# Down-projection of a ConvGLU feed-forward: 38 of its 44 k-tiles by one level of Strassen's algorithm

## The chip, the cores and the metric

One Trainium2 chip, one of its cores. The metric is device time in microseconds from start to end of one execution; lower is better. The three runs of the kernel before have a median of 2918.61 us (2916.6 to 2919.67). Engines are called PE (TensorE, matrix products into PSUM), DVE (VectorE), ACT (ScalarE), POOL (GpSimd) and SP (SyncE, which here issues the transfers).

## The reference

One layer of a streaming encoder: adaLN-modulated RMSNorm, gated linear attention and gated DeltaNet, an output projection, then a ConvGLU feed-forward and a last RMSNorm. The change concerns the second product of the feed-forward and what follows:

```python
D_MODEL = 2048; D_FF = 5632; SEQ = 512; DEC_SEQ = 64

def conv_ffn(h, st, w_up, ffn_conv_w, ffn_conv_b, w_down):
    gate, val = jnp.split(h @ w_up, 2, axis=-1)
    gate_c, new_st = causal_dwconv(gate, st, ffn_conv_w)
    act = jax.nn.silu(gate_c + ffn_conv_b) * val
    return act @ w_down, new_st
...
        f, s_f = conv_ffn(h, ffn_s[l], w_up[l], ffn_conv_w[l], ffn_conv_b[l], w_down[l])
        x = x + g2 * f
...
    y = rmsnorm(x, final_norm)
```

It runs for 512 frames of a prompt and 64 frames of a sample, all in float32. So the down-projection multiplies 576 frames by a matrix of 5632 x 2048.

## The kernel before, in words

Activations lie with the model dimension on the 128 partitions and the frames along the free dimension, in two halves of 288 columns (256 of the prompt, 32 of the sample). w_down falls into 44 k-tiles (128 rows of D_FF) and 16 m-tiles (128 columns of D_MODEL).

A float32 product is made of three products of a reduced type (F32R): each operand is split into a high half (ACT copies it into F32R) and a low half (DVE subtracts the high half from the original). mm6 (L551) does one k-tile of one m-tile for both halves of the frames, six matmuls of 128 x 128 by 128 x 288: high weights with high activations, high weights with low ones, low weights with high ones.

up (L1437) is the stage ahead. It makes 44 tiles of the activation and uses one level of Strassen's algorithm (in Winograd's form) already. For each of the 44 tiles it works through seven products (up_product, L1362), each of 8 pairs of k-tiles and 24 matmuls, and prepares the weights of a product two products ahead (up_prep, L1332: DVE sums of raw weights, then the split by ACT and DVE). The results of a tile pass through buffers "cb", "ca" and "v" for the short convolution (up_conv, L1419) and the gate (up_act, L1425), and are written to DRAM tiles actd.

down (L1480) goes through the 44 k-tiles in 11 groups of four. acts (L1468) loads the four activation tiles of a group from actd into places that the up-projection's operands left free, and splits them; the next group's are loaded in the middle of a group, the first group's before the up-projection ends. For each pair of m-tiles, wtile (L652, through split, L638) loads 4 x 128 x 256 weights (512 KB) and splits them. Each m-tile takes 24 matmuls into a PSUM tile of two banks, of which there are two (pgt, L575), and residual (L1147) then adds the sum, times the adaLN gain, onto x1 in SBUF (two DVE operations, 512 and 64 columns). The 16 tiles of x1 are loaded from DRAM (xd) at the start of down. The eleventh group is done by final (L1511), one half of the frames after the other, with the last RMSNorm (final_part, L1574) between the products.

The order of instructions on each engine is set by a scheduler when the program is built: by the order in which they are written, where an instruction's inputs and buffers are there, and ahead of that order where they are there sooner. So the first activations and weights of down are fetched while up still runs. A buffer of a given tag is handed on when all its readers are done.

## Time and profile before

| | before |
|---|---|
| median of 3 runs | 2918.61 us |
| profiled execution, own time | 2917.59 us |
| its span (first to last instruction) | 2915.8 us |
| mean granted TensorE clock | 0.994 |
| PE instructions (matmuls) | 21052 |
| DVE instructions | 3543 |
| ACT instructions | 2118 |
| DMA traffic | 399.84 MB, 137 GB/s on average |

The span is the stretch of the profiled execution from its first to its last instruction; the execution's own time is 1.8 us longer, and the median of the timed runs 1.0 us longer than that. In the trace, the up-projection's matmuls run from 1311.7 to 2331.5 us, those of the down-projection's first ten groups begin at 2331.7 us, and the last group ends at 2901.5 us. A line number in a group of instructions is that of the kernel before; a busy PE is not a PE at its peak, since matmuls overlap.

### The profile page before, as it was taken

The numbers are of one execution on the slowest core, as the hardware profiler recorded it, in microseconds if no ns is written. First come the engines' busy times: TensorE is split into PE (matmuls) and PEld (weight loads), VectorE is DVE, ScalarE is ACT, GpSimd is POOL, SyncE is SP. The second block draws the span as 40 slices with busy tenths as digits, with TensorE's granted clock in tenths as the row PEclk, the third lists the DMA queues.
The fourth block names the chain that finished last, engine by engine and source line by source line (L and its number), as shares of the span: only waits on it lengthen the run. The fifth ranks groups of instructions, "written<-read, shape, count | busy, mean of one in ns | idle before, by whom it ended". The sixth has DMA issues, their size and how long they took to land.

```text
span 2915.8 us, 52420 instructions
## 1 busy us (share of the span) xinstructions
PE 2865.9 (98%) x21052; PEld 2766.4 (95%) x21052; DVE 2133.5 (73%) x3543; ACT 1239.9 (43%) x2118; POOL 321.0 (11%) x587
## 2 busy tenths in 40 slices
PE   7999999999999999999999999999999999999998
PEld 3599999999999999999999999999999999999997
DVE  5788878777777786468887888887888855555555
ACT  6574566544433233354444444444444422222223
POOL 0015432234210001000000000000000000000000
PEclk8999999999999999999999999999999999999999
DMA  8975555555456548333333333333333553333221
GB/s 302 302 205 148 157 154 159 155 140 165 124 149 174 145 144 250 113 104 106 107 100 105 106 107 106 107 99 106 105 106 107 175 185 102 114 102 113 87 81 66
DMA packets 511879, 399.84 MB, mean 137 GB/s; under 512 B 45865, under 2 KB 437764, under 8 KB 511636
## 3 DMA queue, kind: packets, MB, share of 16 engines
q1 hardware_dynamic: 506212, 385.82, 44.5%
q0 software_dynamic: 5424, 10.68, 1.1%
q8 instruction: 166, 2.72, 0.4%
q14 instruction: 77, 0.63, 0.1%
HBM read 356.27 MB, written 40.13 MB: 136 GB/s over the span
## 4 chain that ended last, share of the span: by engine, by line
PE 90%; DVE 4%; ACT 3%; DMA 2%; issue 1%; POOL 0%; SPq 0%; ACTq 0%; DVEq 0%; POOLq 0%
PE g L560 30%; PE g L562 15%; PE g L1372 9%; PE g L1373 8%; PE g L1374 8%; PE bank L1373 3%; PE bank L1372 3%; PE bank L1374 3%; PE bank L161 1%; DVE acc L819 1%; PE bank L825 1%; PE bank L433 1%; PE bank L752 1%; DVE wl L649 1%; PE bank L756 1%
## 5 line engine op out<-in xcount | busy, mean ns | idle before, releaser
L560 PE MATMUL g<-slot,wh 128*128 128x288 f32 x3168 | 551.4, 295 | 0.2 <-DVE slot L1150 0.2
L1372 PE MATMUL g<-slot,wh 128*128 128x290 f32 x1760 | 533.6, 303 | 3.0 <-ACT p L1384 2.6
L648 ACT ACTIVATE wh<-raw 128x1024 fp32r<-128x1024 f32 x239 | 253.0, 1059 | 658.5 <-PE g L560 622.5
L1373 PE MATMUL g<-slot,wh 128*128 128x290 f32 x1760 | 525.4, 299 | 0.0
L1374 PE MATMUL g<-slot,wl 128*128 128x290 f32 x1760 | 520.6, 296 | 0.0
L560 PEld LDWEIGHTS g<-slot,wh 128*128 128x128 f32 x3168 | 464.5, 188 | 0.7 <-DVE slot L1150 0.5
L560 PE MATMUL g<-hh,wh 128*128 128x288 f32 x1984 | 449.8, 306 | 2.3 <-ACT hh L1159 1.0
L560 PE MATMUL g<-hl,wh 128*128 128x288 f32 x1984 | 431.9, 297 | 0.0
L562 PE MATMUL g<-hh,wl 128*128 128x288 f32 x1984 | 431.5, 298 | 0.0
L1150 DVE SCALAR_TENSOR_TENSOR slot<-g,mod,slot 128x512 f32<-128x512 f32 (+1 forms) x448 | 201.8, 491 | 286.9 <-PE g L562 286.0
L1319 ACT ACTIVATE wh<-raw 128x1024 fp32r<-128x1024 f32 x176 | 186.8, 1061 | 390.2 <-PE g L1373 380.0
L1372 PEld LDWEIGHTS g<-slot,wh 128*128 128x128 f32 x1760 | 331.2, 188 | 17.6 <-ACT p L1384 11.7
L562 PE MATMUL g<-slot,wl 128*128 128x288 f32 x1584 | 341.7, 294 | 0.0
L1374 PEld LDWEIGHTS g<-slot,wl 128*128 128x128 f32 x1760 | 336.5, 191 | 0.0
L1373 PEld LDWEIGHTS g<-slot,wh 128*128 128x128 f32 x1760 | 335.6, 191 | 0.1
L649 DVE TENSOR_TENSOR wl<-raw,wh 128x1024 fp32r<-128x1024 f32 x239 | 291.4, 1220 | 52.2 <-ACT wh L648 51.3
L560 PEld LDWEIGHTS g<-hh,wh 128*128 128x128 f32 x1984 | 318.6, 190 | 5.5 <-ACT hh L1159 1.3
L560 PEld LDWEIGHTS g<-hl,wh 128*128 128x128 f32 x1984 | 320.9, 189 | 0.3
L562 PEld LDWEIGHTS g<-hh,wl 128*128 128x128 f32 x1984 | 319.4, 189 | 0.2 <-issue 0.2
L562 PEld LDWEIGHTS g<-slot,wl 128*128 128x128 f32 x1584 | 255.1, 188 | 0.0
L819 DVE SCALAR_TENSOR_TENSOR acc<-xr,ct,acc 128x512 f32<-128x512 f32 x322 | 230.3, 750 | 1.7 <-DMA xr<-in_w_ada_dram 1.7
L1320 DVE TENSOR_TENSOR wl<-raw,wh 128x1024 fp32r<-128x1024 f32 x176 | 214.7, 1220 | 18.3 <-ACT wh L1319 18.1
(373 smaller groups left out, 4540.5 us busy)
## 6 DMA issues: line engine op xcount, KB each, us to landing
raw<-in_w_up_dram SPq DMA_DIRECT2D x176, 512.0 KB
raw<-in_w_in_dram SPq DMA_DIRECT2D x108, 512.0 KB
raw<-in_w_down_dram SPq DMA_DIRECT2D x88, 512.0 KB
xr<-in_w_ada_dram SPq DMA_DIRECT2D x86, 512.0 KB
ax<-in_w_ada_dram SPq DMA_DIRECT2D x42, 512.0 KB
hraw<-in_w_ada_dram SPq DMA_DIRECT2D x40, 512.0 KB
raw<-in_w_out_dram SPq DMA_DIRECT2D x32, 512.0 KB
slot<-actd SPq DMA_DIRECT2D x44, 288.0 KB
```

Source lines behind the costliest of these rows:

```text
L161: self.nc.tensor.transpose(ps[:, b * P:(b + 1) * P], src4[:, b], self.c["ident"])
L560: T.matmul(ps[:, h if bank is None else bank, :n], wh, x[:, h, :n], start=f, stop=False)
L562: T.matmul(ps[:, h if bank is None else bank, :n], wl, ah[:, h, :n], start=False, stop=stop)
L648: nc.scalar.activation(hi[:, :n_], raw[:, :n_], AF.Copy)
L649: nc.vector.tensor_tensor(lo[:, :n_], raw[:, :n_], hi[:, :n_].bitcast(F32), op=ALU.subtract)
L819: V.scalar_tensor_tensor(acc[s], w[:, k], col, acc[s], op0=ALU.mult, op1=ALU.add)
L1150: self.nc.vector.scalar_tensor_tensor(x1[:, :, z], ps[:, :, c], gain[:, q:q + 1], x1[:, :, z], op0=ALU.mult, op1=ALU.add)
L1319: self.nc.scalar.activation(hi, src, AF.Copy)
L1320: self.nc.vector.tensor_tensor(lo, src, hi.bitcast(F32), op=ALU.subtract)
L1372: T.matmul(ps, wh[:, j], hi, start=(c < 3 and j == 0), stop=False, skip_group_check=True)
L1373: T.matmul(ps, wh[:, j], lo, start=False, stop=False, skip_group_check=True)
L1374: T.matmul(ps, wl[:, j], hi, start=False, stop=(j == NPAIR - 1), skip_group_check=True)
```

## The change

Two k-tiles (FIRST) are done as before, 38 as 19 pairs by Strassen's algorithm, and the last four by final as before. A pair is k-tile 2 + j and k-tile 21 + j; together with the two halves of the frames and the two halves of the m-tiles they make blocks of two by two, which seven products replace where eight would be needed. The pairs come in five groups of 3, 4, 4, 4 and 4; within a group the outputs are done in four quarters (two m-tiles of the upper and two of the lower half), and a quarter takes seven products. A product has n pairs x 2 m-tiles x 3 matmuls (24 with four pairs), summed in one PSUM bank per m-tile.

- Weights: down_load fetches four raw tiles of a quarter; DVE makes four sums of them (down_first, down_prep), and seven splits by ACT and DVE follow (down_split), two products ahead.
- Activations: down_pair makes seven combinations from the two tiles of a pair and splits each (put). The pairs of the next group are made in a group's third and fourth quarter, after the products that the code names. act_load brings activations in through the buffers "cb", "v" and "ca" of the up-projection (stage) and no longer through places of their own.
- Outputs: instead of being scaled and added onto x1 at once, the sums are gathered unscaled in SBUF (acc, and e0 for the part that three of four outputs share) by DVE (down_out). In the last group down_finish loads x from xd (four transfers a call), adds e0, scales by the gain on ACT (g2, negative for the lower half, whose sums have the other sign) and adds x. For the first two k-tiles ACT copies the sums from PSUM to acc.
- final adds its four k-tiles onto acc (final_sum) and reads its outputs there (xf).

```diff
...
 B11, T2, T1, B21, T3, B22, T4 = range(7)
+FIRST, NDOWN, GROUPS = 2, 19, (3, 4, 4, 4, 4)
...
-    def put(self, c, j, src, place=None):
+    def put(self, c, j, src, place=None, w=HZ):
         place = place or self.places.pop(0)
-        t = self.slot(place, F32R)
+        t = self.slot(place, F32R, w)
         self.split_z(t[:, 0], t[:, 1], src)
         self.combos[c, j] = t[:, 0], t[:, 1], place
...
+    def stage(self):
+        n = self.n_stage = self.n_stage + 1
+        tag = ("v", "cb", "v", "ca")[n % 4]
+        return self.ub.tile([P, 2, HZ], F32, tag=tag, bufs=2 if tag == "v" else 1, name=self.name("raw"))[:, :, :HT]
+    def act_load(self, t):
+        raw = self.stage()
+        self.nc.sync.dma_start(raw, self.actd[t])
+        return raw
+    def act_split(self, raw):
+        hh, hl = [self.slot(self.places.pop(0), F32R, HT) for _ in range(2)]
+        self.nc.scalar.activation(hh, raw, AF.Copy)
+        self.nc.vector.tensor_tensor(hl, raw, hh.bitcast(F32), op=ALU.subtract)
+        return hh, hl
+    def pair_load(self, j):
+        return [self.act_load(FIRST + j + half * NDOWN) for half in range(2)]
+    def down_pair(self, j, raws):
+        V = self.nc.vector
+        (b11, b12), (b21, b22) = [(r[:, 0], r[:, 1]) for r in raws]
+        put = lambda c, b: self.put(c, j, b, None, HT)
+        put(B11, b11)
+        V.tensor_tensor(b11, b11, b12, op=ALU.subtract)
+        put(T1, b11)
+        t = self.ub.tile([P, HZ], F32, tag=("p1", "r")[j % 2], name=self.name("t3"))[:, :HT]
+        V.tensor_tensor(t, b22, b12, op=ALU.subtract)
+        V.scalar_tensor_tensor(b12, b11, -1.0, b22, op0=ALU.mult, op1=ALU.subtract)
+        put(T2, b12)
+        put(T3, t)
+        put(B21, b21)
+        V.scalar_tensor_tensor(b21, b12, -1.0, b21, op0=ALU.mult, op1=ALU.subtract)
+        put(B22, b22)
+        put(T4, b21)
+    def down_rows(self, g, half):
+        k = FIRST + half * NDOWN + sum(GROUPS[:g])
+        return k, k + GROUPS[g]
...
+    def down_sum(self, step, c):
+        g, q = step
+        n = GROUPS[g]
+        return self.ua.tile([P, 1024], F32, tag=f"s{c}", name=self.name("s"))[:, :n * 256].rearrange("p (k n) -> p k n", k=n)
+    def down_first(self, step):
+        s1 = self.a[(*step, "s1")] = self.down_sum(step, 1)
+        self.nc.vector.tensor_tensor(s1, self.a[(*step, "a21")], self.a[(*step, "a22")], op=ALU.add)
+    def down_split(self, src):
+        k = src.shape[1]
+        hi, lo = [self.wq.tile([P, 1024], F32R, tag="w" + c, bufs=3, name=self.name("w" + c))[:, :k * 256]
+                  .rearrange("p (k n) -> p k n", k=k) for c in "hl"]
+        self.nc.scalar.activation(hi, src, AF.Copy)
+        self.nc.vector.tensor_tensor(lo, src, hi.bitcast(F32), op=ALU.subtract)
+        return hi, lo
+    def down_prep(self, step, c, following):
+        V, a = self.nc.vector, self.a
+        g = lambda n: a[(*step, n)]
+        if c == 0:
+            w = self.down_split(g("a11"))
+            s2 = a[(*step, "s2")] = self.down_sum(step, 2)
+            V.tensor_tensor(s2, g("s1"), g("a11"), op=ALU.add)
+        elif c == 1:
+            w = self.down_split(g("s2"))
+        elif c == 2:
+            w = self.down_split(g("s1"))
+            if following:
+                self.down_load(following, ("a21", "a22"))
+        elif c == 3:
+            w = self.down_split(g("a12"))
+        elif c == 4:
+            V.tensor_tensor(g("a21"), g("a11"), g("a21"), op=ALU.add)
+            w = self.down_split(g("a21"))
+            if following:
+                self.down_load(following, ("a11", "a12"))
+        elif c == 5:
+            V.tensor_tensor(g("s2"), g("a12"), g("s2"), op=ALU.add)
+            w = self.down_split(g("s2"))
+        else:
+            w = self.down_split(g("a22"))
+            if following:
+                self.down_first(following)
+        a[(*step, "w", c)] = w
+    def down_product(self, step, c):
+        T, (wh, wl) = self.nc.tensor, self.a.pop((*step, "w", c))
+        g = step[0]
+        if c == 0:
+            x, y, z = self.pgt(), self.pgt(), [self.bank() for _ in range(2)]
+            self.sums = x[:, :, :HT], y[:, :, :HT], [b[:, :HT] for b in z]
+            self.banks = [[x[:, a, :HT], y[:, a, :HT], z[a][:, :HT]] for a in range(2)]
+        j0, n = sum(GROUPS[:g]), GROUPS[g]
+        for a in range(2):
+            ps = self.banks[a][(0, 1, 2, 0, 1, 2, 1)[c]]
+            f = slice(a * P, (a + 1) * P)
+            for j in range(n):
+                hi, lo, _ = self.combos[c, j0 + j]
+                T.matmul(ps, wh[:, j, f], hi, start=(c < 3 and j == 0), stop=False, skip_group_check=True)
+                T.matmul(ps, wh[:, j, f], lo, start=False, stop=False, skip_group_check=True)
+                T.matmul(ps, wl[:, j, f], hi, start=False, stop=(j == n - 1), skip_group_check=True)
+    def down_out(self, step, c):
+        V, (g, q) = self.nc.vector, step
+        x, y, z = self.sums
+        if c == 0 and g == 0:
+            self.nc.scalar.activation(self.e0[q], x, AF.Copy)
+            return
+        out = (self.e0[q], self.acc[0, 1][q], self.acc[1, 1][q], self.acc[0, 0][q],
+               self.acc[1, 1][q], self.acc[0, 1][q], self.acc[1, 0][q])[c]
+        if c in (2, 5):
+            for a in range(2):
+                V.tensor_tensor(out[:, a], z[a], out[:, a], op=ALU.add)
+        else:
+            V.tensor_tensor(out, (x, y)[(0, 1, 2, 0, 1, 2, 1)[c]], out, op=ALU.add)
+    def down_finish(self, row, h, q):
+        nc, t = self.nc, self.acc[row, h][q]
+        xt = self.stage()
+        for a in range(2):
+            for c, z in ((slice(0, HP), slice(0, HP)), (slice(HP, HT), slice(ZS, HZ))):
+                nc.sync.dma_start(xt[:, a, c], self.xd[8 * row + 2 * q + a][:, h, z])
+        if row + h:
+            yield
+            nc.vector.tensor_tensor(t, t, self.e0[q], op=ALU.add)
+        yield
+        for a in range(2):
+            for n, c in enumerate((slice(0, HP), slice(HP, HT))):
+                nc.scalar.activation(t[:, a, c], t[:, a, c], AF.Copy, scale=self.g2[:, 8 * row + 2 * q + a, n:n + 1])
+        yield
+        nc.vector.tensor_tensor(t, t, xt, op=ALU.add)
     def down(self):
+        A = self.nc.scalar
         free = [self.combos[c, j][2] for c in range(7) for j in range(NPAIR)]
         take = lambda n: [free.pop(0) for _ in range(n)]
...
+        self.combos, self.a, self.n_stage = {}, {}, 0
         self.raw = self.raw_late
...
+        self.places = firsts = take(2 * FIRST)
+        firsts = list(firsts)
+        acts = [self.act_split(self.act_load(k)) for k in range(FIRST)]
+        self.places = take(7 * GROUPS[0])
+        quarters = lambda places: [self.slot(p, F32, HT) for p in places]
+        self.acc = {}
+        for row in range(2):
+            for h in range(2):
+                self.acc[row, h] = quarters(take(4))
+        self.e0_places = take(4)
+        self.e0 = quarters(self.e0_places)
+        self.places += free + firsts
+        self.g2 = self.sp.tile([P, KD, 2], F32, tag="g2", bufs=1, name="g2")
+        for half, f in ((0, 1.0), (1, -1.0)):
+            A.activation(self.g2[:, 8 * half:8 * half + 8], self.mod[:, 5, 8 * half:8 * half + 8], AF.Copy, scale=f)
+        steps = [((g, q), c) for g in range(len(GROUPS)) for q in range(4) for c in range(7)]
+        blocks = [b for b, c in steps if c == 0] + [None]
+        prep = lambda n: self.down_prep(*steps[n], blocks[n // 7 + 1]) if n < len(steps) else None
+        raws = {0: self.pair_load(0)}
+        for m0 in range(0, KD, 4):
+            wh, wl = self.wtile(self.i["w_down"][0, :FIRST * P, m0 * P:(m0 + 4) * P].rearrange("(k p) n -> p k n", p=P))
+            if m0 == 4:
+                self.down_load(blocks[0], ("a21", "a22"))
+            if m0 == 8:
+                self.down_load(blocks[0], ("a11", "a12"))
+                self.down_first(blocks[0])
+            for m in range(m0, m0 + 4):
+                ps = self.pgt()
+                c = slice((m - m0) * P, (m - m0 + 1) * P)
+                for k in range(FIRST):
+                    self.mm6(ps, wh[:, k, c], wl[:, k, c], acts[k], k == 0, k == FIRST - 1)
+                for h in range(2):
+                    A.activation(self.acc[m // 8, h][m % 8 // 2][:, m % 2], ps[:, h, :HT], AF.Copy, scale=(1.0, -1.0)[m // 8])
+            j = m0 // 4
+            if j < GROUPS[0]:
+                raws[j + 1] = self.pair_load(j + 1)
+                self.down_pair(j, raws.pop(j))
+        for n in range(2):
+            prep(n)
+        j, last, tasks = GROUPS[0], len(GROUPS) - 1, []
+        acts, loads = [], list(range(NFF - 4, NFF))
+        for n, (step, c) in enumerate(steps):
+            g, q = step
+            prep(n + 2)
+            self.down_product(step, c)
+            self.down_out(step, c)
+            if q == 3:
+                self.places += [self.combos[c, sum(GROUPS[:g]) + i][2] for i in range(GROUPS[g])]
+            if g < last and (q, c) in ((2, 0), (3, 1), (3, 3), (3, 5)):
+                if j + 1 < NDOWN:
+                    raws[j + 1] = self.pair_load(j + 1)
+                self.down_pair(j, raws.pop(j))
+                j += 1
+            if g == last:
+                if q == 0 and c < 4:
+                    loads[c] = self.act_load(loads[c])
+                if q == 0 and 1 < c < 6:
+                    acts.append(self.act_split(loads[c - 2]))
+                if c > 2:
+                    tasks.append(self.down_finish(*((0, 0), (1, 1), (0, 1), (1, 0))[c - 3], q))
+                for t in tasks[:2]:
+                    if next(t, self) is self:
+                        tasks.remove(t)
+        for t in tasks:
+            for _ in t:
+                pass
+        self.final(acts, self.places + [])
...
+    def xf(self, m, h):
+        return self.acc[m // 8, h][m % 8 // 2][:, m % 2]
+    def final_sum(self, ps, m, h):
+        x = self.xf(m, h)
+        for n, c in enumerate((slice(0, HP), slice(HP, HT))):
+            self.nc.vector.scalar_tensor_tensor(x[:, c], ps[:, m % 2, c], self.mod[:, 5, m, n:n + 1], x[:, c], op0=ALU.mult, op1=ALU.add)
...
+        free += self.e0_places
...
-                self.residual(ps[:, m % 2:m % 2 + 1], self.x1[m][:, h:h + 1], self.mod[:, 5, m])
+                self.final_sum(ps, m, h)
...
```

46 lines of the change are left out of this document (13 added, 33 removed).

## The prediction

> **What bounds the kernel now.** I read the page first (busy time and the chain that ended last), then the table of stretches for the two stages that the change joins, then the waits inside the down-projection.
>
> ```profile
> span 2915.8 us, 52420 instructions
> ...
> PE 2865.9 (98%) x21052; PEld 2766.4 (95%) x21052; DVE 2133.5 (73%) x3543; ACT 1239.9 (43%) x2118; POOL 321.0 (11%) x587
> ...
> PE 90%; DVE 4%; ACT 3%; DMA 2%; issue 1%; POOL 0%; SPq 0%; ACTq 0%; DVEq 0%; POOLq 0%
> ```
>
> TensorE carries 90% of the chain. In the stretches below the columns are stretch, length, PE, PEld, DVE, ACT and POOL busy, the granted clock, DMA share and GB/s. The first row lies in the up-projection, which already uses one level of Strassen, the second in the down-projection of today.
>
> ```profile
> 1800.00:2000.00 200.00, 200.00 (x1462) 197.02 (x1461) 163.17 (x200) 89.69 (x106) 15.16 (x27) 1.00 0.37 106
> 2500.00:2600.00 100.00, 100.00 (x759) 100.00 (x758) 53.28 (x88) 22.03 (x24) 0.00 (x0) 1.00 0.35 109
> ```
>
> TensorE never rests in either. VectorE and ScalarE wait for it (us in total, times, longest):
>
> ```profile
> ACT wh L648 <- PE g L560: 340.7, 67, 5.3
> DVE slot L1150 <- PE g L562: 222.4, 135, 2.2
> ```
>
> So a removed matmul is worth its full pitch, as long as VectorE, 53% busy here and 82% in the up-projection, can pay for it.
>
> **What is removed.** The down-projection has 44 x 16 x 6 = 4224 matmuls. After the change there are 2 x 16 x 6 = 192 (two k-tiles first), 19 pairs x 4 quarters x 7 products x 2 x 3 = 3192, and 384 (four k-tiles last): 3768, so 456 go. 759 matmuls per 100 us make 0.132 us each: **60.2 us**. The rest of the change gives some of it back.
>
> **Pace of a product.** A product sums into one PSUM bank through a run of matmuls, as the up-projection does; today two banks alternate.
>
> ```profile
> 2013.60 0.30 PE L1373 MATMUL g<-slot,wh 128*128 128x290 f32 x1
> ...
> 2016.56 0.29 PE L1374 MATMUL g<-slot,wl 128*128 128x290 f32 x1
> ```
>
> These are the second and the last of one product's 24: 22 pitches in 2.96 us, 0.1345 us at 290 columns, 0.1336 at 288. If that is the pace, 3192 x 0.0016 = **5 us** are lost (0 if it is the alternating pace). I take 5, the row with the same order of work.
>
> **VectorE in the five groups.** These groups of instructions give the durations (x count, then busy us, mean ns, and idle time before them):
>
> ```profile
> L1320 DVE TENSOR_TENSOR wl<-s,wh 128x1024 fp32r<-128x1024 f32 x132 | 161.0, 1220 | 2.2 <-ACT wh L1319 0.4
> L1319 ACT ACTIVATE wh<-s 128x1024 fp32r<-128x1024 f32 x132 | 140.2, 1062 | 114.2 <-PE bank L1373 87.6 <-DVE wl L1320 15.4 <-PE g L1373 8.0
> L1330 DVE TENSOR_TENSOR s<-raw,raw 128x1024 f32<-128x1024 f32 x44 | 53.7, 1219 | 1.0 <-DMA raw<-in_w_up_dram 1.0
> L1403 DVE TENSOR_TENSOR v<-v,sqa 128x580 f32<-128x580 f32 x44 | 33.6, 763 | 1.5
> L1390 DVE TENSOR_TENSOR r<-bank,p 128x290 f32<-128x290 f32 x44 | 19.9, 452 | 0.0
> L1224 DVE TENSOR_TENSOR slot<-slot,slot 128x290 fp32r<-128x290 f32 x44 | 19.1, 456 | 8.3 <-ACT slot L1223 8.1
> L1223 ACT ACTIVATE slot<-slot 128x290 fp32r<-128x290 f32 x44 | 18.0, 439 | 6.2 <-DVE slot L1231 2.9 <-DVE slot L1224 1.1 <-POOL slot L1206 0.6
> L1555 DVE TENSOR_TENSOR hw<-raw,hw 128x512 fp32r<-128x512 f32 x10 | 6.8, 685 | 4.7 <-ACT hw L1554 4.7
> L1475 ACT ACTIVATE slot<-slot 128x576 fp32r<-128x576 f32 x44 | 30.1, 683 | 36.3 <-PE g L562 28.5 <-DMA slot<-actd 3.6 <-PE g L1374 2.3
> ```
>
> Where VectorE's work lies dense, an instruction starts before the one ahead has ended:
>
> ```profile
> 2000.32 1.23 DVE L1339 TENSOR_TENSOR s<-s,raw 128x1024 f32<-128x1024 f32 x1 [0.85 <-DMA raw<-in_w_up_dram]
> 2001.46 1.22 DVE L1320 TENSOR_TENSOR wl<-raw,wh 128x1024 fp32r<-128x1024 f32 x1
> ...
> 2003.73 0.45 DVE L1395 TENSOR_TENSOR v<-g,r 128x290 f32<-128x290 f32 x1
> 2004.10 1.22 DVE L1320 TENSOR_TENSOR wl<-raw,wh 128x1024 fp32r<-128x1024 f32 x1
> ...
> 2009.49 0.76 DVE L1403 TENSOR_TENSOR v<-v,sqa 128x580 f32<-128x580 f32 x1
> 2010.17 1.22 DVE L1320 TENSOR_TENSOR wl<-s,wh 128x1024 fp32r<-128x1024 f32 x1
> ```
>
> So I charge start to start: 1.14 us for 1024 columns, 0.37 for 290, 0.68 for 580, and for 768 the middle of 685 and 1220 ns less the same overlap, 0.87.
>
> A block (one quarter of the outputs, four pairs, seven products) costs VectorE 7 low halves and 4 weight sums of 1024, 11 x 1.14 = 12.5, and the outputs, 5 of 576 and 4 of 288, 3.4 + 1.5: 17.4 us. TensorE needs 168 x 0.1336 = 22.4. Making a pair of activations for the next group (down_pair) is 7 low halves and 4 sums of 288: 11 x 0.37 and a little for the two three-operand ones, 4.3 us; four of them fall in a group. A full group is 4 x 17.4 + 17.2 = 86.8 us of VectorE against 89.6 of TensorE: enough on average, but three of the four pairs lie in the last block. There VectorE needs 17.4 + 12.9 = 30.3 against 22.4, 7.9 us too much; weights are prepared two products (6.4 us) ahead, so at best 1.5 us of TensorE time are lost. Written order gives the other end: from the second product of that block on, six products (19.2 us) face five outputs (3.5), three pairs (12.9) and the weights of five products with four sums (10.3), 26.7 us: 7.5 lost. I take 4 for each of groups 1 to 3, nearer to the low end, since the up-projection runs at 82% VectorE without a rest of TensorE and pairs whose data are there can slip into earlier gaps. Group 0 has three pairs a block: 13.8 us of VectorE (its first outputs go to ScalarE) against 126 x 0.1336 = 16.8; its last block is 26.7 against 16.8, less a lead of 4.8: 5.1 at best, 10 by written order; I take 7. The last group makes no pairs, but rescales: 7 operations of 576 a quarter, 4.8 us, so 22.2 against 22.4, and four activation splits: 2 (0 to 5). Together **21 us** (10 to 38). ScalarE (7 high halves of 1.06 a block, 28 of 0.44 a group) stays near half.
>
> **The join.** Today the activations of the first k-tiles are loaded long before the up-projection ends. Now the first of them (act_load through stage) goes into the buffer "cb", which up_conv of the last tile still reads.
>
> ```profile
> 2331.52 0.30 PE L1374 MATMUL g<-slot,wl 128*128 128x290 f32 x1
> 2331.66 0.70 PE L560 MATMUL g<-slot,wh 128*128 128x288 f32 x4
> ```
> ```profile
> 2332.63 0.81 DVE L1422 SCALAR_TENSOR_TENSOR ca<-cb,cols,ca 128x578 f32<-128x578 f32 x1
> ```
> ```profile
> 2308.34 2.79 DMA slot<-actd
> ...
> 2313.35 5.15 DMA slot<-actd
> ```
>
> TensorE goes on without a gap today, at 2331.66. With the change "cb" is free at 2333.4; a load of this size took 2.8 and 5.2 us on the chain; ScalarE's high half takes 0.68: first matmul at 2336.9 to 2339.3, 5.3 to 7.6 us late. Behind that load on SyncE wait the pairs' loads, whose buffers come free later still; they are needed only 25 us on, when the 192 matmuls are done. I take 6. Such a rest has a second price:
>
> ```profile
> 1315.00:1320.00 5.00, 2.08 (x17) 1.88 (x17) 5.00 (x13) 4.01 (x10) 2.70 (x2) 1.00 0.90 242
> 1320.00:1325.00 5.00, 5.00 (x25) 4.50 (x24) 3.31 (x9) 1.27 (x3) 0.10 (x1) 0.66 0.35 97
> 1325.00:1330.00 5.00, 5.00 (x40) 5.00 (x39) 4.66 (x10) 3.76 (x7) 0.00 (x0) 1.00 0.23 60
> ```
>
> After some 3 us without work the granted clock was 0.66 for one stretch, 25 matmuls instead of 40, 2 us lost. So the join costs **8 us** (5 to 10). The Trainium skill ("TensorE: Matmul & The Clock Gate", section on the HAM clock gate) states half the clock after an idle window of about 3.4 us until a busy one has passed; that is 1.7 us by an estimate from its figures, and the row agrees.
>
> **The rest.** In the 25 us of the first two k-tiles ScalarE must empty PSUM (32 of 288 columns) and make 21 high halves, about 24 us of work: 1 us (0 to 4). The residual's loads move from the start to the last group and become 64 DMAs; today ten of them take SyncE half a microsecond each, so 16 a quarter make 8 us beside 22:
>
> ```profile
> 2320.49 5.30 SPq L1490 DMA_DIRECT2D slot<-xd  x10
> ```
>
> They cost nothing while those 22 us cover them; the weight loads behind them, issued a product or more ahead, would otherwise come late by the excess. Weight bytes are the same. The last stage keeps its matmuls; up to 4.8 us of rescaling of the last quarter now overlap its start: 1 us (0 to 3).
>
> **Sum.** 60.2 - 5 - 21 - 8 - 1 - 1 = 24 us. The profiled execution took 2917.6 us (span 2915.8), 1 us below the median of the runs, 2918.6; from the median that is **2894 us**, 0.8% faster. With all low costs it is 2874, with all high ones 2919. About 0.2% (5.8 us) is what a measurement here can tell from no change.
>
> **Rivals.** (B) VectorE bounds the groups: the written order is kept, pairs go ahead of weights, and the bursts cost 38: 2894 + 17 = 2911. For it: 97% load in a full group and a written order that puts the pair ahead of the next weights. The same comes out if an operation held VectorE for its full duration: 4 x (11 x 1.22 + 5 x 0.76 + 4 x 0.45) + 4 x 11 x 0.46 = 96.3 us against 89.6, 6.7 lost in each of three groups, 14 in group 0, 36 with the last. Against: the up-projection loses nothing at 82%, and 1.14 us lie between starts of operations of 1.23 us. The rule for that second way is the Trainium skill's ("VectorE: DVE Perf Modes", section "The DRAIN you can't avoid": the next operation starts only when the pipe is empty); the rows above differ from it, and the section says itself that an operation that isn't held starts earlier. (C) Slower than before: in a pair the two halves run by turns, ScalarE then VectorE, because each sum waits for both halves of the one before. A pair then holds VectorE for 7 x (0.44 + 0.46) + 4 x 0.46 = 8.1 us; groups 1 to 3 lose 4 x 8.1 - 20 each, group 0 4 x 8.1 - 12, together 58 and 2 for the last: 2894 + 39 = 2933. It decides from 7.2 us a pair on, where the bursts reach 45. Against: in L1224's row the same halves waited 8.1 us for ScalarE in 44 times, 0.2 each, so 5.6 a pair at most. (D) Pairs fit wholly into earlier gaps, the pace stays 0.132: 2874. (E) The stalls of a burst come in pieces of 3 us, and the clock falls after each: two a group, four groups, 2 us each: 2894 + 16 = 2910; against it, VectorE catches up while the clock is low. That the clock gate of the page named above acts here at all is shown by the 0.66; that it acts within groups no row shows.
>
> **Chances.** Forecast 0.50 (own range 2880 to 2908), B 0.17, C 0.15, D 0.10, E 0.08. Faster by over 0.2%: 0.49 of the forecast, all of D, 0.10 of B and E, 0.69. Slower: 0.14 of C and 0.01 of B, 0.15. Within: 0.16. The range 2870 to 2922 leaves out most of C and a little below D.
>
> **What would show it.** Matmuls 456 fewer; a TensorE gap of 5 to 8 us where the down-projection begins, with the clock below 1 after it; VectorE 9 tenths or more in the groups, TensorE's waits for low halves only in each group's last block and the first product after it. Wrong, if TensorE waits throughout the blocks, if a pair occupies VectorE for over 7 us, or if the gap at the join exceeds 12 us.

## The result and the profile after

| | before | after |
|---|---|---|
| median of 4 runs | 2917.61 us (2916.59 to 2919.67) | 2889.86 us (2883.68 to 2891.70) |
| profiled execution, own time | 2917.59 us | 2889.40 us |
| span | 2915.8 us | 2887.6 us |
| mean granted clock | 0.994 | 0.991 |

The ratio is 0.990 (95% interval 0.9883 to 0.9917). The page of the kernel after: its instructions, VectorE in 40 slices, and the chain that ended last.

```profile
span 2887.6 us, 52030 instructions
...
PE 2814.7 (97%) x20596; PEld 2713.3 (94%) x20596; DVE 2304.2 (80%) x3742; ACT 1357.9 (47%) x2379; POOL 320.9 (11%) x587
...
DVE  5788888777778787468887888888888879999995
...
PE 84%; DVE 7%; DMA 4%; ACT 3%; issue 1%; SPq 0%; POOL 0%; ACTq 0%; DVEq 0%; POOLq 0%
```

VectorE in the same 40 slices before:

```profile
DVE  5788878777777786468887888887888855555555
```

21052 - 20596 = 456 matmuls are gone, as counted. VectorE fills its slices in the Strassen groups (the run of 9s at the end, where 5s stood), and TensorE's share of the chain fell from 90% to 84%: it now rests in places where it never did. The timeline of TensorE after, every rest of over half a microsecond and the first matmul of each stretch (start, length, instruction, and in brackets the rest ahead of it and what ended it; a row may join several matmuls):

```profile
2341.36 0.85 PE L561 MATMUL g<-slot,wh 128*128 128x288 f32 x2 [8.88 <-ACT slot L1484]
...
2366.61 0.67 PE L561 MATMUL g<-slot,wh 128*128 128x288 f32 x3 [0.76 <-ACT slot L1665]
...
2369.90 0.30 PE L1590 MATMUL g<-slot,wh 128*128 128x288 f32 x1
...
2441.86 0.40 PE L1590 MATMUL g<-slot,wh 128*128 128x288 f32 x1 [0.65 <-DVE slot L1607]
...
2532.87 0.40 PE L1590 MATMUL g<-slot,wh 128*128 128x288 f32 x1 [1.94 <-DVE slot L1607]
...
2625.72 0.40 PE L1590 MATMUL g<-slot,wh 128*128 128x288 f32 x1 [1.93 <-DVE slot L1607]
...
2716.74 0.41 PE L1590 MATMUL g<-slot,wh 128*128 128x288 f32 x1 [1.71 <-DVE slot L1607]
...
2802.53 0.38 PE L1775 MATMUL bank<-consts,fs 128*88 128x128 f32 x2
...
2811.92 0.47 PE L1787 MATMUL bank<-consts,slot 128*128 128x128 f32 x1 [5.83 <-DVE slot L1714]
```

Three kinds of rest are to be seen: one long one at the join (8.88), four short ones at the boundaries of the groups, and one long one in the last stage (5.83). The stretches between these rows make the budget. Up ends at 2341.36 - 8.88 = 2332.48, 0.8 later than the 2331.66 of before. Before, the first ten groups run from there to the last stage's first matmul, in TensorE's timeline before:

```profile
2839.47 0.38 PE L1569 MATMUL bank<-consts,fs 128*88 128x128 f32 x2
```

- From up's end to the last stage: before 507.8 us for 3840 matmuls (0.1322 each), after 470.1 for 3384. At the old pitch these need 447.5, so 60.3 us were saved and 22.6 given back: 12.0 in the join with the first two k-tiles (37.4 us for 192 matmuls that need 25.4) and 10.5 in the Strassen groups (432.6 for 422.1).
- From there to the end of the span: before 76.3 us, after 85.1: 8.8 given back.
- 60.3 - 12.0 - 10.5 - 8.8 - 0.8 = 28.2 us, the difference of the spans.

The clock shows what the rests cost beyond themselves. The table of stretches after (stretch, length, PE, PEld, DVE, ACT, POOL busy, granted clock, DMA share, GB/s):

```profile
2335.00:2340.00 5.00, 0.00 (x0) 0.00 (x0) 4.35 (x8) 1.55 (x3) 0.00 (x0) 0.53 0.73 223
2340.00:2345.00 5.00, 3.64 (x15) 3.59 (x16) 2.00 (x4) 1.57 (x3) 0.00 (x0) 0.50 0.69 198
2345.00:2350.00 5.00, 5.00 (x38) 5.00 (x37) 4.55 (x13) 4.72 (x15) 0.00 (x0) 0.94 0.24 67
2530.00:2535.00 5.00, 3.06 (x17) 2.83 (x17) 5.00 (x8) 1.85 (x3) 0.00 (x0) 0.83 0.41 118
2810.00:2815.00 5.00, 3.08 (x13) 3.02 (x14) 5.00 (x12) 2.76 (x7) 0.00 (x0) 0.50 0.08 20
2815.00:2820.00 5.00, 5.00 (x34) 5.00 (x33) 4.24 (x11) 0.00 (x0) 0.00 (x0) 0.84 0.00 0
```

After the join 3.64 us at half clock and 5 at 0.94 lose some 2 us, after the last stage's rest 3.08 at half and 5 at 0.84 another 2. At one boundary the clock showed 0.83 in two stretches, 1.7 us lost.

**The join.** Why 8.88 and not 6? VectorE and then the queue of SyncE and ScalarE, each in its timeline after:

```profile
2336.07 0.45 DVE L1225 TENSOR_TENSOR slot<-raw,slot 128x288 fp32r<-128x288 f32 x1
2336.44 0.82 DVE L1423 SCALAR_TENSOR_TENSOR ca<-cb,cols,ca 128x578 f32<-128x578 f32 x1
```
```profile
2337.34 0.53 SPq L1478 DMA_DIRECT2D raw<-actd  x1
```
```profile
2340.62 0.69 ACT L1484 ACTIVATE slot<-raw 128x576 fp32r<-128x576 f32 x1 [2.55 <-DMA raw<-actd]
```

The path is the one forecast: up_conv's last reading of "cb", the load into "cb", the high half, the first matmul. But up_conv's reading came at 2336.44, 4.0 us after up's end, where before it came 1.0 after (2332.63 against 2331.66): the change's new work stood ahead of it in VectorE's queue. The low half of a pair in the row above (L1225), a low half of an activation tile (L1485) and two sums of weights of 768 columns (L1535, L1552) take 2.8 us there from start to start.

**The last stage.** Timeline of VectorE after, ahead of the first addition of final_sum (L1714), which the rest of 5.83 us waited for:

```profile
2806.01 1.23 DVE L650 TENSOR_TENSOR wl<-raw,wh 128x1024 fp32r<-128x1024 f32 x1 [1.83 <-ACT wh L649]
2807.22 0.76 DVE L1624 TENSOR_TENSOR slot<-slot,raw 128x576 f32<-128x576 f32 x1
2807.90 0.75 DVE L1618 TENSOR_TENSOR slot<-slot,slot 128x576 f32<-128x576 f32 x1
2808.57 0.75 DVE L1624 TENSOR_TENSOR slot<-slot,raw 128x576 f32<-128x576 f32 x1
...
2810.71 0.76 DVE L1624 TENSOR_TENSOR slot<-slot,raw 128x576 f32<-128x576 f32 x1
2811.38 0.48 DVE L1714 SCALAR_TENSOR_TENSOR slot<-g,mod,slot 128x256 f32<-128x256 f32 x1
```

Lines 1618 and 1624 are down_finish's additions for the last quarters, written ahead of final. TensorE has done the stage's first two m-tiles (24 matmuls). The next instruction in its queue is a transposition for the norm (L1787, the last row of TensorE's timeline above), which reads what this addition writes, so it waits until VectorE comes to it. The four rescaling additions in these rows take 2.7 us from start to start. Beside them stand low halves of weights (the first, in the top row, had waited 1.83 us for ScalarE) and a copy.

### The profile page after: what moved, and what is told of

Read it like the earlier page. It is cut to its first block, busy times and chain, and to the rows that moved or that the text cites. A ratio compares the mean times of both kernels' runs of the same rounds, so it can differ in the third digit from the quotient of the medians.

```text
span 2887.6 us, 52030 instructions
## 1 busy us (share of the span) xinstructions
PE 2814.7 (97%) x20596; PEld 2713.3 (94%) x20596; DVE 2304.2 (80%) x3742; ACT 1357.9 (47%) x2379; POOL 320.9 (11%) x587
## 4 chain that ended last, share of the span: by engine, by line
PE 84%; DVE 7%; DMA 4%; ACT 3%; issue 1%; SPq 0%; POOL 0%; ACTq 0%; DVEq 0%; POOLq 0%
PE g L561 18%; PE g L563 9%; PE g L1373 9%; PE g L1374 8%; PE g L1375 8%; PE bank L1374 3%; PE bank L1373 3%; PE bank L1375 3%; PE g L1590 3%; PE g L1592 3%; PE g L1591 3%; DVE acc L820 1%; PE bank L1592 1%; PE bank L162 1%; PE bank L1590 1%
## 5 line engine op out<-in xcount | busy, mean ns | idle before, releaser
L1320 ACT ACTIVATE wh<-raw 128x1024 fp32r<-128x1024 f32 x176 | 186.7, 1061 | 396.0 <-PE g L1374 391.7
L1373 PEld LDWEIGHTS g<-slot,wh 128*128 128x128 f32 x1760 | 331.1, 188 | 17.0 <-ACT p L1385 11.6
L1375 PEld LDWEIGHTS g<-slot,wl 128*128 128x128 f32 x1760 | 336.3, 191 | 0.0
L1374 PEld LDWEIGHTS g<-slot,wh 128*128 128x128 f32 x1760 | 334.8, 190 | 0.1
L649 ACT ACTIVATE wh<-raw 128x1024 fp32r<-128x1024 f32 x163 | 172.6, 1059 | 315.5 <-PE g L561 278.6
L650 DVE TENSOR_TENSOR wl<-raw,wh 128x1024 fp32r<-128x1024 f32 x163 | 198.9, 1222 | 55.2 <-ACT wh L649 53.5
L1590 PE MATMUL g<-slot,wh 128*128 128x288 f32 x760 | 225.4, 297 | 6.5 <-DVE slot L1607 6.5
L1321 DVE TENSOR_TENSOR wl<-raw,wh 128x1024 fp32r<-128x1024 f32 x176 | 214.7, 1220 | 18.8 <-ACT wh L1320 18.7
L1592 PE MATMUL g<-slot,wl 128*128 128x288 f32 x760 | 224.7, 296 | 0.0
L1591 PE MATMUL g<-slot,wh 128*128 128x288 f32 x760 | 224.5, 295 | 0.0
L1374 PE MATMUL bank<-slot,wh 128*128 128x290 f32 x704 | 210.1, 298 | 0.0
L1373 PE MATMUL bank<-slot,wh 128*128 128x290 f32 x704 | 209.4, 297 | 0.0
```

The source lines that it names most:

```text
L650: nc.vector.tensor_tensor(lo[:, :n_], raw[:, :n_], hi[:, :n_].bitcast(F32), op=ALU.subtract)
L1320: self.nc.scalar.activation(hi, src, AF.Copy)
L1321: self.nc.vector.tensor_tensor(lo, src, hi.bitcast(F32), op=ALU.subtract)
L1373: T.matmul(ps, wh[:, j], hi, start=(c < 3 and j == 0), stop=False, skip_group_check=True)
L1374: T.matmul(ps, wh[:, j], lo, start=False, stop=False, skip_group_check=True)
L1375: T.matmul(ps, wl[:, j], hi, start=False, stop=(j == NPAIR - 1), skip_group_check=True)
```

## The experiments

The theory after the result: three separate losses, each with its own mechanism: (1) the join, because the first activations pass through a buffer that up still reads; (2) the last stage, because leftover rescaling stands ahead of the first additions; (3) the boundaries of the groups, because of the pairs. The rival for all of them: VectorE is simply at its limit from the join on, and a rest that is cured in one place comes up in another.

The table has the stretches of every kernel from its profiled execution, read off TensorE's timeline as above. Up's end varies between 2323.6 and 2334.4 us, ahead of the stage that the edits concern, so the stretches behind it tell more than the whole time. "After, again" is the unchanged kernel run beside the three kernels that follow it in the table (ratio interval 0.9865 to 0.9904). Ratios are to the kernel before.

| kernel | median us | ratio | join and first k-tiles | Strassen groups | last stage to end | sum |
|---|---|---|---|---|---|---|
| after | 2889.86 | 0.9900 | 37.4 | 432.6 | 85.1 | 555.1 |
| after, again | 2883.58 | 0.9885 | 37.8 | 430.5 | 85.1 | 553.3 |
| own places | 2879.06 | 0.9864 | 27.5 | 435.0 | 83.9 | 546.4 |
| rescaling later | 2878.37 | 0.9865 | 37.5 | 433.4 | 78.4 | 549.3 |
| both | 2868.50 | 0.9832 | 27.1 | 430.9 | 78.6 | 536.6 |
| no pairs made | 2875.37 | 0.9849 | 37.9 | 423.0 | 82.7 | 543.7 |
| two additions more a block | 2891.15 | 0.9905 | 37.3 | 431.5 | 87.3 | 556.2 |
| seven more a block | 2957.11 | 1.0128 | 37.2 | 498.8 | 86.8 | 622.8 |
| banks by turns | 2888.33 | 0.9896 | 37.4 | 434.5 | 83.6 | 555.5 |
| sums change places | 2879.69 | 0.9877 | 37.2 | 429.0 | 85.1 | 551.3 |
| last pair earlier | 2882.75 | 0.9881 | 37.8 | 428.8 | 85.7 | 552.2 |
| both, and sums change places | 2863.19 | 0.9823 | 26.7 | 430.8 | 78.3 | 535.8 |
| both, and last pair earlier | 2868.22 | 0.9838 | 27.6 | 431.2 | 78.2 | 536.9 |

**The join: own places for the first two activation tiles.**

```diff
-        acts = [self.act_split(self.act_load(k)) for k in range(FIRST)]
+        own, acts = take(FIRST), []
+        for k in range(FIRST):
+            raw = self.slot(own[k], F32, HT)
+            self.nc.sync.dma_start(raw, self.actd[k])
+            acts.append(self.act_split(raw))
...
-        self.places += free + firsts
+        self.places += free + firsts + own
```

> The first two activation tiles are loaded into two places of their own instead of the buffers cb and v. Theory A (TensorE bounds the stage and loses time at three places): the gap of 8.9 us at the join, the rest of 0.8 behind it and some 2 us of low clock go, 10 to 12 us faster than the changed kernel, ratio near 0.986. Rival B (VectorE's amount of work bounds the stage): the pairs of group 0 come late instead and TensorE waits there, less than 4 us faster.

Measured: 2879.06 us, ratio 0.9864 (0.9844 to 0.9883), 4.5 us below the unchanged kernel beside it. TensorE's timeline at the join:

```profile
2329.65 0.30 PE L1375 MATMUL g<-slot,wl 128*128 128x290 f32 x1
2329.79 0.30 PE L561 MATMUL g<-slot,wh 128*128 128x288 f32 x1
...
2357.33 0.40 PE L1590 MATMUL g<-slot,wh 128*128 128x288 f32 x1 [0.78 <-ACT slot L1669]
```

The down-projection's first matmul follows up's last after one pitch, and this stretch is 9.9 to 10.3 us shorter, as expected. The time fell by less. In the profiled execution the Strassen groups took 435.0 us: two of its boundary rests lowered the clock (0.85 and 0.81, then 0.66 in stretches of 5 us, 3.4 us in all), where one and none did in the two profiles of the unchanged kernel. So the cause of the join's loss is shown; in this execution nearly half of the gain was eaten by another term, which the profile of both cures did not have. Of the other executions only the times are known.

**The last stage: rescaling after the first additions.**

```diff
-        for t in tasks:
-            for _ in t:
-                pass
+        self.left = [t[1] for t in sorted(tasks, key=lambda t: t[0])]
...
# final, first half of the frames, after final_sum of each m-tile:
+                if self.left and next(self.left[0], self) is self:
+                    self.left.pop(0)
```

(tasks now carries the half of the frames; what is left is drained before the second half.)

> What is left of the rescaling when the last product is written goes one step behind each m-tile of the last stage instead of ahead of it. Theory A: the rest of 5.8 us at the start of the last stage comes from VectorE doing this rescaling ahead of the sums that free PSUM; it goes with its 2 us of low clock, 5 to 8 us faster than the changed kernel. Rival: the rest comes from the transfers of that moment (DMA share 1.00 between 2800 and 2805 us), so at most 1 us.

Measured: 2878.37 us, ratio 0.9865 (0.9846 to 0.9884), 5.2 below the unchanged kernel. TensorE's waits from 2800 us on, all there are (us in total, times, longest):

```profile
PE g L561 <- ACT wh L649: 0.5, 1, 0.5
PE g L561 <- DVE slot L1713: 0.5, 2, 0.2
```

The rest of 5.8 to 6.5 us is gone, and the last stage is 6.7 us shorter (78.4 for 85.1). The same rescaling is done, later, so it was the order. That order is VectorE's and with it TensorE's: the scheduler now puts the first transposition behind 36 matmuls of the stage in place of 24, and the run does not separate the two. The transfers, the rival, are as dense as before: the DMA share from 2800 to 2805 us is 1.01, against 1.00 in the kernel after. Of the 8.8 us given back in this stage 2.1 remain: 1.0 in these two waits, some 0.75 behind the last matmul (13.3 us from its start to the end of the span, 12.6 before), and a remainder that is not traced.

**Both.** The two edits together.

> Both edits together. Theory A: the two gains add up, 15 to 20 us faster than the changed kernel, 2870 to 2875 us, ratio near 0.984. Rival B: less than 6 us.

Measured: 2868.50 us, ratio 0.9832 (0.9813 to 0.9851), 15.1 below the unchanged kernel and faster than both kernels. The stretches show 27.1 and 78.6 us: the two cures add up, and nothing came up elsewhere (430.9 in the groups). The rival falls for these two losses.

**No pairs made.** Does the making of the pairs cause the rests at the boundaries, and what is that worth?

```diff
-                hi, lo, _ = self.combos[c, j0 + j]
+                hi, lo, _ = self.combos[c, j % 3]
...
-                if j + 1 < NDOWN:
-                    raws[j + 1] = self.pair_load(j + 1)
-                self.down_pair(j, raws.pop(j))
```

> Left out: the loads, combinations and splits of the 16 pairs of groups 1 to 4; their products read group 0's combinations again. The number of matmuls and all work on weights and outputs stay. Theory A: the rests of TensorE at the group boundaries (6.5 us) and their low clock (1.7) go, 7 to 9 us faster than the changed kernel. Rival B: 16 times 4.2 us of VectorE are gone, 20 us or more faster.

Measured: 2875.37 us, ratio 0.9849 (0.9831 to 0.9867). No rest is left in the groups, which take 423.0 us, 7.5 to 9.6 less than in the two profiles of the kernel after. The last stage is 2.4 us shorter too (its long rest is 3.98 us). So the making of the pairs costs 7.5 to 9.6 us in the groups. The run leaves out all of it, VectorE's sums and low halves, ScalarE's high halves and the loads, so it does not say which of these counts. It also gives the pace of a product without rests: 423.0 / 3192 = 0.1325 us a matmul.

**Two, and seven, additions more in each block.** How much room has VectorE? Each added operation is of 580 columns into a tile that nobody reads, after the products named.

```diff
+        if c in (1, 4):        # the other kernel: all seven products
+            junk = self.ub.tile([P, 2, HZ], F32, tag="g", name=self.name("junk"))
+            V.tensor_tensor(junk, self.rb, self.rb, op=ALU.add)
```

> Two more VectorE operations of 580 columns in each of the 20 blocks (into a buffer that nobody reads), 27 us of VectorE in all. Theory A: a full group has 92.2 us of VectorE instead of 86.8, against 91 us that it takes now, so the slack takes up about half: 10 to 18 us slower than the changed kernel. Rival B: 27 us slower. A third way, VectorE has room: under 4 us.

> Seven more such operations in each block, 95 us of VectorE in all. What the time grows by less than 95 us is VectorE's slack in the five groups. Theory A: 70 to 82 us slower than the changed kernel (slack of some 4 us a group, and of the rests at the join). Rival B: 93 to 97.

Measured: 2891.15 us (0.9905, 0.9885 to 0.9926) and 2957.11 us (1.0128, 1.0107 to 1.0149). VectorE in the table of stretches, over the groups, for the unchanged kernel again, then two more, then seven more (these rows begin and end with the groups):

```profile
2366.00:2797.00 431.00, 424.84 (x3198) 423.36 (x3197) 409.82 (x575) 201.49 (x305) 0.00 (x0) 1.00 0.43 127
```
```profile
2366.00:2797.00 431.00, 424.73 (x3192) 422.69 (x3192) 426.74 (x606) 200.96 (x305) 0.00 (x0) 1.00 0.42 126
```
```profile
2372.00:2870.00 498.00, 450.07 (x3190) 439.06 (x3189) 487.54 (x701) 200.75 (x306) 0.00 (x0) 0.96 0.37 111
```

Forty operations more, 27 us at 0.67 from start to start, left the groups at 431.5 us (430.5 and 432.6 without) and put 2 us onto the last stage. But they wait for no other operation, and the scheduler put nine of them ahead of the groups, into the join. So 31 ran in the groups, 21 us, and two operations of the rescaling moved out to the last stage. VectorE was idle for 21 of the 431 us before and is busy in 427 of them now. A hundred beyond these cost 498.8 - 431.5 = 67.3 us, about their full price: 91 of the 96 more that the trace holds ran in the groups, 61 us, and VectorE's own idle time there grew by 6. So my expectation that two a block would cost some 10 us fell: VectorE had about 20 us of room in the groups, and only what exceeds it is paid. With seven more, TensorE's waits (us in total, times, longest) are those of a stage that VectorE bounds, the prediction's rival B:

```profile
PE g L1590 <- DVE slot L1607: 24.7, 12, 4.4
PE g L1590 <- ACT wh L1541: 10.0, 7, 2.3
PE g L1592 <- DVE wl L1542: 9.2, 12, 0.9
```

**Banks by turns.** Is the pace of a product set by its summing into one bank? The loops over the pairs and the two m-tiles change places.

```diff
-        for a in range(2):
-            ps = self.banks[a][(0, 1, 2, 0, 1, 2, 1)[c]]
-            f = slice(a * P, (a + 1) * P)
-            for j in range(n):
-                hi, lo, _ = self.combos[c, j0 + j]
+        for j in range(n):
+            hi, lo, _ = self.combos[c, j0 + j]
+            for a in range(2):
+                ps = self.banks[a][(0, 1, 2, 0, 1, 2, 1)[c]]
+                f = slice(a * P, (a + 1) * P)
```

> In a product the two m-tiles take turns, so that consecutive groups of three matmuls go to two PSUM banks instead of one. If the bank sets the pitch (0.1327 us against 0.1318), 2 to 3 us faster than the changed kernel; if not, within 1 us.

Measured: 2888.33 us, ratio 0.9896 (0.9877 to 0.9915), no difference. The same stretch of the groups, in the table of stretches of the kernel after, by turns, and before:

```profile
2450.00:2530.00 80.00, 80.00 (x608) 80.00 (x607) 75.83 (x111) 37.00 (x53) 0.00 (x0) 1.00 0.40 121
```
```profile
2450.00:2530.00 80.00, 80.00 (x605) 80.00 (x604) 76.00 (x110) 35.15 (x49) 0.00 (x0) 1.00 0.40 124
```
```profile
2450.00:2530.00 80.00, 80.00 (x607) 80.00 (x606) 40.59 (x69) 16.32 (x17) 0.00 (x0) 1.00 0.31 99
```

605 to 608 matmuls of 288 columns in 80 us in all three: the order of the banks does not set the pace.

**The boundaries: is it the order, or the work?** Product 6 of a block and product 1 of the next share their banks, so VectorE must add up product 6 within one product. The first edit lets the two sums change places in every second block, the second makes the last pair one product earlier.

```diff
# sums change places (down_product, and down_out accordingly)
-            self.sums = x[:, :, :HT], y[:, :, :HT], [b[:, :HT] for b in z]
+            z = [b[:, :HT] for b in z]
+            x, y = x[:, :, :HT], y[:, :, :HT]
+            self.sums = (x, z, y) if (4 * g + step[1]) % 2 else (x, y, z)
...
```
```diff
# last pair earlier
-            if g < last and (q, c) in ((2, 0), (3, 1), (3, 3), (3, 5)):
+            if g < last and (q, c) in ((2, 0), (3, 1), (3, 3), (3, 4)):
```

> Question: are the rests at the group boundaries (6.7 us in six rests, and one clock loss of 1.7) a lack of VectorE time, or only the order in which PSUM is handed over? In the changed kernel the sum with products 1, 4 and 6 lies in one pair of banks, and the next block's product 1 takes the same banks, so product 6 has to be added up by VectorE within the 3.2 us of one product. Here the sums with products 1, 4, 6 and with 2, 5 change places in every second block, so the banks of product 6 are next needed by product 2, 6.4 us later. No work is left out. Theory A (handover): the rests on line 1607 fall below 1.5 us in sum, the stretch from the first Strassen product to the last stage from 430.5-432.6 to 424-426 us, the time by 6-8 us. Rival (VectorE is short of time in a group's last block): the rest moves on to another product, the stretch stays above 429 us, the time within 2 us.

> The last pair of the next group is made one product earlier in a group's last block, after product 4 in place of 5; nothing else changes and no work is left out. Theory A (handover: what counts is how much VectorE work stands ahead of product 6's addition in its queue): the pair's pieces stand ahead of product 5's addition, whose bank has more room; the rests at the boundaries at least halve (3.5 us or less in sum), the time falls by 3-5 us. Rival (the sum of the work in the last block is too much): the rests stay at 5-7 us or move, the time within 2 us.

Measured: 2879.69 us (0.9877, 0.9859 to 0.9896) and 2882.75 us (0.9881, 0.9867 to 0.9896), both ratios within the interval of the unchanged kernel (0.9865 to 0.9904). With the sums changing places TensorE's waits in the groups (us in total, times, longest) are

```profile
PE g L1594 <- DVE wl L1542: 3.4, 5, 1.0
PE g L1592 <- DVE slot L1609: 1.1, 1, 1.1
```

(line 1609 is the addition of outputs, 1607 in the kernel after). The wait for product 6's addition is gone from the boundaries, and in its place TensorE waits there for the low half of the next weights, which comes from the same VectorE: 4.5 us in all, for 6.0 to 6.7. The groups took 429.0 us, which lies on the rival's line and far from the 424 to 426 of theory A. The last pair made earlier splits the rests into pieces of 0.4 us, 2.9 in all, so they halve as its theory A says, but the groups still take 428.8. To tell chance from gain, each was added to the two cures:

> All three cures together: the first two activation tiles in places of their own, the rescaling after the first additions of the last stage, and the two sums changing places in every second block. No work is left out. If the three losses (join 10, last stage 6-8, boundaries 6-8) are separate, the time is 6-8 us below that of the first two cures alone: about 0.981 of the kernel before, some 2859 on 2916. Rival (they overlap, or VectorE's time is then the limit): within 2 us of the two cures, 0.983.

> The first two cures (own places for the first two activation tiles, rescaling after the first additions of the last stage) with the last pair of a group made one product earlier. No work is left out. With the two cures alone the Strassen stretch was 430.9 us with 5.2 us of rests; the earlier pair alone had 428.8 us with 2.8. If the earlier pair relieves the boundary whatever else is changed: rests 3 us or less, the stretch 427-429, some 2-4 us below the two cures (ratio 0.982). Rival (its gain was chance, as with the exchanged sums, which did nothing on top of the two cures): stretch 430-432, rests about 5 us, ratio 0.983 or more.

Measured: 2863.19 us (0.9823, 0.9807 to 0.9840) and 2868.22 us (0.9838, 0.9821 to 0.9855), against 0.9832 for the two cures alone; the groups took 430.8 and 431.2 us, against 430.9. The rival holds here: neither did anything more on top of the cures that these runs can tell. In the first of them the rest stands at the weights again, the longest one in TensorE's waits at 1.7 us:

```profile
PE g L1594 <- DVE wl L1542: 4.6, 5, 1.7
```

The pieces hide why. The profile counts a rest from the modelled end of a matmul, 0.30 us after its start, while the next one would start after 0.13; so a rest costs 0.17 us more than its length, and a delay below that does not show. Counted from start to start (what a step exceeds 0.132 us by, for steps of over 0.16), the delays in the groups are 7.8 us in the unchanged kernel (again), 6.3 and 6.1 with the two edits, and 7.8 with both cures, 7.7 and 8.1 with one of the edits on top of them.

So a change of order at the boundaries moved the rest to another operand or split it; only leaving the pairs out was shown to help. That the amount of VectorE's work is the cause is not wholly shown, for VectorE itself waits at these boundaries. ScalarE and VectorE ahead of the rest at 2532.87 in the kernel after:

```profile
2527.23 0.45 ACT L1224 ACTIVATE slot<-raw 128x288 fp32r<-128x288 f32 x1 [1.07 <-PE g L1592]
```
```profile
2528.71 0.46 DVE L1225 TENSOR_TENSOR slot<-raw,slot 128x288 fp32r<-128x288 f32 x1 [1.15 <-ACT slot L1224]
...
2532.07 0.75 DVE L1607 TENSOR_TENSOR slot<-g,slot 128x576 f32<-128x576 f32 x1
```

A low half of a pair waits for its high half on ScalarE, which had waited for TensorE, and the addition that ends the rest (L1607) comes behind it in VectorE's queue. VectorE waits so for 0.9 to 1.2 us ahead of three of the four boundary rests, in both profiles of the unchanged kernel. It is not the whole cause: with both cures and the earlier pair these waits come to 0.7 us in the groups, and the stretch is no shorter. No run takes them out alone. Whether fewer or cheaper operations for a pair would help, or a pair spread over earlier blocks (the free places, eight at the start of each group after the first, do not hold a second pair there), was not tried.

## Why the prediction was right, and where its terms were off

The time, 2889.86 us, lies 4 us from the forecast of 2894. The saving and the three places of loss were right. The sizes of the losses were not, and that they cancelled is luck.

**60.2 us for 456 matmuls: right.** The budget gives 60.3.

**Pace of a product, 5: too high.** 3192 x (0.1325 - 0.132) = 1.6 us by the kernel without pairs. The row of 290 columns that I scaled from was no measure of summing into one bank: by turns and in one bank go at the same pace. Why 290 columns take 0.1345 where 288 take 0.132 stays open.

**Bursts in the five groups, 21: too high, 7.5 to 9.6 (range 10 to 38).** This is the step that was furthest off. The total of VectorE's work was right: by my charges it is 4 x 13.8 + 17.2 + 3 x 86.8 + 4 x 22.2 = 421.6 us over the groups, and the row above has 409.8 busy in 431, with pair pieces done ahead of it and rescaling left behind it. What failed is the assumption that the pairs stay near their written place. The table of stretches after, for the low halves of line 1225 alone (stretch, length, VectorE busy and count, clock, DMA share, GB/s): up to the groups, in group 0, and in the stretches of about a block's length that end with the rests behind groups 0 and 1. A piece that runs across a border counts on both sides.

```profile
2300.00:2370.00 70.00, 13.87 (x34) 0.93 0.45 135
2370.00:2424.00 54.00, 1.25 (x4) 1.00 0.36 107
2424.00:2442.00 18.00, 5.55 (x13) 1.00 0.41 121
...
2510.00:2533.00 23.00, 8.02 (x19) 1.00 0.46 132
```

Group 0 itself needs 21 such pieces; 34 were begun ahead of 2370. Of the 28 pieces for group 1, 13 fell into the stretch that ends group 0, where I had put 21; the other 15 were done earlier, 13 of them even before group 0 began. The boundary's rest is 0.65 us, where I had priced 7. For the next group 19 fell into that stretch, and the rests are 1.7 to 1.9, near my lower bound of 1.5 and not the 4 that I took. The last group, priced at 2, has no rest of over 0.3 us.

The wait is another one, too. I had TensorE run out of low halves of weights, which are prepared two products ahead. It waits for the addition of product 6 (line 1607), which hands back the banks that the next block's product 1 needs. The low halves come next: TensorE waits for them when the sums change places.

**The join, 8, and the first two k-tiles, 1: together 9, measured 12.0.** The mechanism is shown (own places take 10 us off). I placed up_conv's last reading where the trace of before has it, and overlooked that the change queues its own VectorE work ahead of it: 4.0 us after up's end in place of 1.0. In the first two k-tiles TensorE waited 0.76 us for ScalarE, as forecast.

**The last stage, 1 (0 to 3): 8.8 measured, the other large miss.** I had the rescaling of the last quarter overlap the stage's start, 4.8 us of it, but priced it as if TensorE could run on. It can't: after 24 matmuls the next instruction in its queue is a transposition of the first output, and VectorE comes to that output's addition only after the rescaling written ahead of it. A rest of 5.83 us and the low clock behind it are the price. The run with the rescaling later shows that this order costs 6.7; of the other 2.1 us, 1.0 stands in short waits.

**Sum.** 36 us of losses forecast, 32.1 measured (12.0 + 10.5 + 8.8 + 0.8), so the time came out 4 us below the forecast. The bursts and the pace were over-priced by some 15 to 17 us, the join and the last stage under-priced by 11: the total is better than its terms.

**The rivals.** B (VectorE bounds the groups): no, TensorE's waits stand at four boundaries, and forty operations more cost 2 us; a hundred beyond that make B's profile. C (pairs by turns, slower): hardly; in the groups VectorE waits for ScalarE's half in a pair only four times, 4.3 us in all, about once a boundary. D (all hidden): no, but its 0.132 a matmul was nearer than my 0.1336. Its 2874 was the sum with all low costs, 10 us of bursts among them; with the pairs wholly hidden and my other terms it would have been 2868. E (the clock falls after bursts): once, 1.7 us; other executions of variants show it up to twice.

## What to carry to other kernels

When a change moves work onto an engine with room, price the handovers apart from the average: here some 20 us of room in the groups did not help at the join and in the last stage. There a buffer still in use and a few operations written ahead of the one that TensorE waited for cost 10 and 7 us. Look for what the change queues in front of the steps that already ended the old stage, and move leftover work behind the first hand-back. And count delays from start to start: here two changes of order at the boundaries moved the rests to another operand or split them, and saved nothing on top of the other cures.

## What the runs showed of the hardware

The clock fell after rests shorter than I had assumed. Of six boundary rests of 1.85 to 2.1 us in the profiles of the kernel after and its variants without added work, five lowered the granted clock (0.83 over two stretches of 5 us after one of 1.94; 0.66 over one after 1.89), and of nine between 1.65 and 1.8 one did; each time it cost 1.7 us. The Trainium skill ("TensorE: Matmul & The Clock Gate", section "What's actually happening") states the half clock after at least one idle window of about 3.4 us. The 0.50 after rests of 8.9 and 5.8 us agrees with that; the falls after 1.9 us differ from it, and the measurement decides.

In the kernel with two additions more a block, each added operation takes 752 ns on VectorE; behind 35 of the 40 the next one started 0.67 us after the start of the added one. The Trainium skill ("VectorE: DVE Perf Modes", section "The DRAIN you can't avoid") has the next operation start only when the pipe is empty, and adds that one that isn't held starts earlier. The trace agrees with the addition, as in the prediction's rows.
